# Mixer B of a two-layer encoder: probabilities times values as split products with the values' two parts in one 128-column operand

## The chip, the cores and the metric

The kernel runs on one core of a Trainium2 chip. The metric is the device time of one launch in microseconds (us); lower is better. Engines are named as in the profile: PE is the TensorE matmul engine and PEld its weight loads, DVE is VectorE, ACT is ScalarE, POOL is GpSimd, SP issues most DMAs. Each engine runs its own instructions strictly in the order in which they were written, and waits at the head of its queue until what that instruction reads is there.

## The reference, cut to what matters

Two layers of the same form run over a sequence of 512 tokens with 1024 features. A layer projects its input `u` with one wide matrix into mixer A (dilated windows), mixer B (grouped attention), gates and merge gates; the two mixers' outputs are projected, merged, projected again and normalised. The change is in mixer B: 8 query heads share 2 key/value heads of 64 features, and every query sees all 512 keys.

```
def one_block(qblk):
    logits = jnp.einsum('bqkge,bske->bkgqs', qblk, k, preferred_element_type=jnp.float32) * (HEAD_DIM ** -0.5)
    p = jax.nn.softmax(logits, axis=-1).astype(v.dtype)
    return jnp.einsum('bkgqs,bske->bqkge', p, v)
```

All data are 32-bit floats. The kernel computes most products in a rounded 32-bit type (`fp32r`, F32R in the code) that PE takes at full rate: it splits each operand into a rounded high part and the low part that is left, and adds two or three products of parts.

## The kernel before

**Weights.** The fill work of a layer is one stream of weight chunks. A chunk is split in four pieces by `split_piece`: ACT copies a piece of `raw` into `wh` (L175, rounds it), DVE subtracts to get `wl` (L176). One piece is emitted after each unit of fill work (`tick`), a chunk ahead of its use. Units are 12 matmuls of 512 columns (`feature_unit`) or 24 of 256 columns (`token_chunk`), on `uh`, `ul`, `wh`, `wl`, all through the helper `mm` at L90.

**Mixer B** (`mixer_b`) has 16 passes per layer, one per block of 128 queries and pair of heads (e = 0, 1). In each pass

- Q transposes the query block (L613); ACT and DVE make its two parts `qst` (L615, L616),
- L multiplies them with the keys into `L` (128 x 1024 in PSUM); DVE takes the row maximum (L631) and scales it (L634); ACT takes the exponentials of both halves with their sums (L637); DVE inverts the sums (L639) and scales both halves (L641),
- T transposes the probabilities in eight 128x128 blocks into `T` (L663); ACT copies `T` to `pt` (L665),
- V multiplies: for each of the 4 key blocks and each head of the pair one plain 32-bit matmul with a 64-column stationary block of `v`, 128 columns of `pt` moving, the two heads in the two halves of the output's partitions; DVE copies the 128x128 result to `ys` (L655).

**Order.** `pipeline` writes the passes as T(i), Q(i+2), L(i+1), fill, V(i), fill. `weave` puts in between 1.1 units of fill for every step of the mixer, so that most passes carry two units and every fifth carries three. The order on every engine is the order of emission; nothing is sorted later. On DVE a pass therefore reads: row maximum, its scaling, inversion, two scalings, a `wl` piece, the copy of V, now and then the rotation of a query block (L492, L501) or four steps of the adaLN sums (L281, L283), or in layer 1 the normalisation's affine (L1298, L1299), then another `wl` piece, `qst`, and the next row maximum.

**Values.** `b_copy_kv` evacuates keys (`xk`) and values (`v`) of all token blocks from the projection's PSUM result with two ACT copies (L518). In layer 0 it runs once for 4 blocks, right before the key rotation on DVE starts (`k_rotate`: L476 and on, `k_scale`: L543), whose result PE transposes at L597 (`b_keys`). In layer 1 it runs twice for 2 blocks each.

**Buffers.** `pt` has two buffers, `T` and `L` one each, small PSUM results four banks `b` (`B1`).

Of the kernel before, what the change touches and what calls it, by code (L numbers as in the profile page):

```python
# [11 lines left out]
F32 = mybir.dt.float32  # L12
F32R = mybir.dt.float32r
AF = mybir.ActivationFunctionType
# [24 lines left out]
def trunk_kernel(ctx, tc, x, c, rel_table, ln_g, ln_b, w_ada, b_ada, w_in, b_gate,  # L39
                 q_norm_g, k_norm_g, w_pa, w_pb, w_o, rope, buckets, out):  # L40
    nc = tc.nc
    pe, act, dve, pool, sp = nc.tensor, nc.scalar, nc.vector, nc.gpsimd, nc.sync
# [5 lines left out]
    ring = ctx.enter_context(tc.tile_pool(name="ring", bufs=2))  # L48
# [7 lines left out]
    def fresh(p):  # L56
        uid[0] += 1
        return f"{p}{uid[0]}"
# [21 lines left out]
    G = Slots(one, "g", NG, [128, 512])  # L80
    B1 = Slots(psum, "b", 4, [128, 512])

    def big(tag):
        return psum.tile([128, 1024], F32, tag=tag, name=fresh(tag))
# [4 lines left out]
    def mm(o, l, r, start, stop):  # L89
        pe.matmul(o, l, r, start=start, stop=stop, skip_group_check=True)  # L90
# [123 lines left out]
    idn = one.tile([128, 128], F32, name="idn")  # L214
# [255 lines left out]
    small = ring  # L470
# [41 lines left out]

    def b_copy_kv(r0, nr, o, st):

        if "v" not in st:
            st["v"], st["xk"] = G.get(), G.get()
        for n, c in (("xk", 0), ("v", 128)):
            act.activation(st[n].rearrange("p (r d) -> p r d", r=4)[:, r0:r0 + nr], o[:, :, c:c + 128], AF.Copy)  # L518

    def b_copy_q(ch, rp, o, st):  # L520
        xq = st["xq", ch, rp] = G.get()
# [83 lines left out]
    def mixer_b(st, ys):  # L605
        subs = [(2 * rp + r, 2 * ch + hp) for rp in range(2) for ch in range(2) for r in range(2) for hp in range(2)]

        def Q(i):
            r, hp = subs[i]
            qd = st["qd", hp // 2, r].rearrange("p (h f) -> p h f", h=4)  # L610
            o = B1.get()
            for e in range(2):
                pe.transpose(o[:, 128 * e:128 * e + 128], qd[:, 2 * (hp % 2) + e], idn)  # L613
            q = small.tile([128, 2, 256], F32R, tag="qst", name=fresh("qst"))
            act.activation(q[:, 0], o[:, 0:256], AF.Copy)  # L615
            dve.tensor_sub(q[:, 1], o[:, 0:256], q[:, 0].bitcast(F32))  # L616
            B1.put(o)
            st["q", i] = q
            if hp % 2:
                G.put(st["qd", hp // 2, r])  # L620

        def L(i):
            q_factors(st)
            r, hp = subs[i]
            ks, q = st["ks", hp // 2], st.pop(("q", i))
            lg = big("L")
            for e in range(2):
                for j in range(2):
                    mm(lg[:, 512 * e:512 * e + 512], q[:, j, 128 * e:128 * e + 128], ks, j == 0, j == 1)
            sm = small.tile([128, 3, 2], F32, tag="bst", name=fresh("bst"))  # L630
            dve.tensor_reduce(out=sm[:, 0], in_=lg.rearrange("p (e k) -> p e k", e=2), op=OP.max, axis=AX.X, negate=True)  # L631
            at = 16 * (hp // 2) + 4 * r + 2 * (hp % 2)
            f = st["qn"][:, 1, at:at + 2]
            dve.tensor_mul(sm[:, 0], sm[:, 0], f)  # L634
            p = tmp4("s")
            for e in range(2):
                act.activation(p[:, 512 * e:512 * e + 512], lg[:, 512 * e:512 * e + 512], AF.Exp,  # L637
                               scale=f[:, e:e + 1], bias=sm[:, 0, e:e + 1], accum_out=sm[:, 1, e:e + 1])
            dve.reciprocal(sm[:, 2], sm[:, 1])  # L639
            for e in range(2):  # L640
                dve.tensor_scalar(p[:, 512 * e:512 * e + 512], p[:, 512 * e:512 * e + 512], sm[:, 2, e:e + 1], None, op0=MUL)  # L641
            st["p", i] = p

        def T(i):
            st["pt", i] = transpose_p(st.pop(("p", i)))

        def V(i):
            r, hp = subs[i]
            pt = st.pop(("pt", i)).rearrange("p (e k q) -> p e k q", e=2, k=4)
            v = st["v"].rearrange("p (r h d) -> p r h d", r=4, h=2)  # L650
            o = B1.get()
            for k in range(4):
                for e in range(2):
                    mm(o[64 * e:64 * e + 64, 0:128], v[:, k, hp // 2], pt[:, e, k], k == 0, k == 3)
            dve.tensor_copy(ys[hp][:, 128 * r:128 * r + 128], o[:, 0:128])  # L655
            B1.put(o)

        yield from pipeline(len(subs), Q, L, T, V, lambda i: True, st["more"])

    def transpose_p(p):  # L660
        t = big("T")
        for j in range(8):
            pe.transpose(t[:, 128 * j:128 * j + 128], p[:, 128 * j:128 * j + 128], idn)  # L663
        pt = tmp4("pt")
        act.activation(pt, t, AF.Copy)  # L665
        return pt
# [619 lines left out]
    for l in range(DEPTH):  # L1286
# [30 lines left out]
        def main():  # L1317
            yield from b_prepare(st, deque([keep] * 8 if l else []))
            yield from mixer_b(st, yb)
            b_done["b"] = True  # L1320
            G.put(st["v"], st["ks", 0], st["ks", 1])
            yield from mixer_a(st, 0, ya, deque([lambda: None] * 4 + [lambda: load_bias(st, 1)]))
            yield from mixer_a(st, 1, ya)

# [73 lines left out]
```

## Time and profile before

| | us |
|---|---|
| median of 3 runs | 1197.84 (1197.66 to 1198.01) |
| the profiled execution, own time | 1199.13 |
| its span, first to last instruction | 1197.0 |
| PE busy in the span | 1163.0 |
| DVE busy | 675.4 |
| ACT busy | 531.1 |

Mixer B occupies about 80 to 230 us (layer 0) and 660 to 810 us (layer 1) of the span. A busy time is the union of an engine's instructions. A matmul's shown duration includes its passage through the array; what it costs in a full stream is the distance from its start to the next one's start. On DVE too, an instruction may start a little before the one ahead of it has ended, and its price in a row of instructions is the distance of starts.

### The profile page before, as it was taken

Reading aid. Unit: us, or ns where it says so; the run is one execution under the profiler, and the core shown is the slowest. Engines: PE = TensorE matmul, PEld = TensorE weight load, DVE = VectorE, ACT = ScalarE, POOL = GpSimd, SP = SyncE. Lnnn points to the kernel's source line nnn. Section 1 sums busy time; section 2 is a strip of 40 time slices with the busy share of each in tenths; the row PEclk is TensorE's granted clock in tenths of the full one; section 3 lists DMA queues with packets and bytes.
Section 4 is the critical chain, followed back from the end, with each engine's and each line's share of the span. In section 5 each row is a group of like instructions: output and inputs, shape, how many; then the busy total and the mean of one; then the engine's idle time right before and its main releaser. Section 6 shows DMA issues by size and latency. Waiting matters only on the chain.

```text
span 1197.0 us, 19187 instructions
## 1 busy us (share of the span) xinstructions
PE 1163.0 (97%) x7491; PEld 998.2 (83%) x7491; DVE 675.4 (56%) x1582; ACT 531.1 (44%) x1112; POOL 54.0 (5%) x85
## 2 busy tenths in 40 slices
PE   7899999999999999999989999999999999999996
PEld 6888888888887787888989888888878778888896
DVE  6776766655455365336755667664333533843477
ACT  2364544444554454323275545544554553533320
POOL 0021000001000000000002001000000000000000
PEclk9999999999999999999999999999999999999998
DMA  9935433546343243334522326335232223323331
GB/s 280 294 116 150 123 109 117 150 133 185 103 128 120 59 129 96 90 104 150 170 71 71 114 91 182 112 107 167 83 114 85 88 73 114 116 88 106 123 107 71
DMA packets 161314, 146.31 MB, mean 122 GB/s; under 512 B 8942, under 2 KB 149078, under 8 KB 161224
## 3 DMA queue, kind: packets, MB, share of 16 engines
q1 hardware_dynamic: 159176, 139.71, 38.5%
q0 software_dynamic: 2048, 5.38, 1.9%
q8 instruction: 59, 0.97, 0.3%
q14 instruction: 31, 0.25, 0.1%
HBM read 134.87 MB, written 8.62 MB: 120 GB/s over the span
## 4 chain that ended last, share of the span: by engine, by line
PE 88%; DVE 6%; ACT 2%; DMA 1%; issue 1%; SPq 1%; POOL 0%; DVEq 0%; ACTq 0%
PE b L90 75%; PE L L90 6%; PE T L663 5%; DVE acc L283 1%; PE T L90 1%; DMA raw<-in_w_ada_dram 1%; PE b L613 1%; DVE wl L176 1%; ACT g L948 0%; DMA s<-in_w_in_dram 0%; SPq L999 0%; DVE g L1252 0%; DVE g L1258 0%; ACT g L1271 0%; DVE wl L1023 0%
## 5 line engine op out<-in xcount | busy, mean ns | idle before, releaser
L176 DVE TENSOR_TENSOR wl<-raw,wh 128x512 fp32r<-128x512 f32 x304 | 205.1, 687 | 286.1 <-ACT wh L175 286.1
L90 PE MATMUL b<-uh,wh 128*128 128x512 f32 x768 | 308.4, 402 | 0.6 <-ACT g L423 0.6
L90 PE MATMUL b<-uh,wl 128*128 128x512 f32 x768 | 299.5, 390 | 1.7 <-DVE wl L176 1.7
L90 PE MATMUL b<-ul,wh 128*128 128x512 f32 x768 | 300.0, 391 | 0.0
L175 ACT ACTIVATE wh<-raw 128x512 fp32r<-128x512 f32 x304 | 179.9, 622 | 32.7 <-issue 24.8
L90 PEld LDWEIGHTS b<-uh,wh 128*128 128x128 f32 x768 | 144.0, 188 | 43.6 <-issue 12.0
L90 PEld LDWEIGHTS b<-uh,wl 128*128 128x128 f32 x768 | 144.2, 188 | 33.8 <-DVE wl L176 2.5
L90 PEld LDWEIGHTS b<-ul,wh 128*128 128x128 f32 x768 | 144.3, 188 | 27.6
L90 PE MATMUL b<-wh,uh 128*128 128x256 f32 x416 | 120.8, 290 | 0.0
L90 PE MATMUL b<-wl,uh 128*128 128x256 f32 x416 | 117.7, 283 | 0.0
L90 PE MATMUL b<-wh,ul 128*128 128x256 f32 x416 | 117.6, 283 | 0.0
L665 ACT ACTIVATE pt<-T 128x1024 f32<-128x1024 f32 x64 | 65.4, 1022 | 73.3 <-PE T L663 70.3
L738 ACT ACTIVATE s<-s,ast 128x256 f32<-128x256 f32 x128 | 63.5, 497 | 68.3 <-DVE ast L733 62.9
L283 DVE SCALAR_TENSOR_TENSOR acc<-raw,sc,acc 128x256 f32<-128x256 f32 x168 | 81.3, 484 | 8.4 <-DMA raw<-in_w_ada_dram 3.2
L90 PEld LDWEIGHTS b<-wh,uh 128*128 128x128 f32 x416 | 79.5, 191 | 4.8 <-issue 3.6
L90 PEld LDWEIGHTS b<-wl,uh 128*128 128x128 f32 x416 | 79.5, 191 | 0.8 <-DVE wl L176 0.2
L90 PEld LDWEIGHTS b<-wh,ul 128*128 128x128 f32 x416 | 79.4, 191 | 0.0
L90 PE MATMUL b<-g,wh 128*128 128x512 f32 x256 | 79.2, 391 | 0.0
L637 ACT ACTIVATE s<-L,bst,qn 128x512 f32<-128x512 f32 x64 | 49.2, 773 | 65.9 <-DVE bst L634 65.9
L90 PE MATMUL b<-wh,g 128*128 128x256 f32 x384 | 71.4, 284 | 0.7 <-DVE g L1191 0.5
L90 PE MATMUL b<-pt,g 128*64 128x128 f32 x1024 | 70.0, 279 | 0.0
L90 PEld LDWEIGHTS b<-pt,g 128*64 128x64 f32 x1024 | 54.6, 136 | 17.7 <-issue 13.7
(177 smaller groups left out, 1615.5 us busy)
## 6 DMA issues: line engine op xcount, KB each, us to landing
raw<-in_w_in_dram SPq DMA_DIRECT2D x126, 512.0 KB, 4.1
raw<-in_w_ada_dram SPq DMA_DIRECT2D x96, 256.0 KB, 3.9
raw<-in_w_o_dram SPq DMA_DIRECT2D x16, 512.0 KB
g<-in_x_dram SPq DMA_DIRECT2D x16, 256.0 KB, 5.5
vph<-g SPq DMA_DIRECT2D x16, 256.0 KB, 2.1
g<-vph SPq DMA_DIRECT2D x16, 256.0 KB, 6.0
g<-frow SPq DMA_DIRECT2D x32, 128.0 KB, 3.1
raw<-in_w_pa_dram SPq DMA_DIRECT2D x8, 512.0 KB, 3.5
```

What stands on the lines that cost most here:

```text
L90: pe.matmul(o, l, r, start=start, stop=stop, skip_group_check=True)
L175: act.activation(hi[:, d], raw[:, s], AF.Copy)
L176: dve.tensor_sub(lo[:, d], raw[:, s], hi[:, d].bitcast(F32))
L283: dve.scalar_tensor_tensor(a, raw[:, k], col, a, op0=MUL, op1=ADD)
L613: pe.transpose(o[:, 128 * e:128 * e + 128], qd[:, 2 * (hp % 2) + e], idn)
L637: act.activation(p[:, 512 * e:512 * e + 512], lg[:, 512 * e:512 * e + 512], AF.Exp, scale=f[:, e:e + 1], bias=sm[:, 0, e:e + 1], accum_out ...
L663: pe.transpose(t[:, 128 * j:128 * j + 128], p[:, 128 * j:128 * j + 128], idn)
L665: act.activation(pt, t, AF.Copy)
L738: act.activation(p4[:, e, b], p4[:, e, b], AF.Exp, bias=sm[:, e, b:b + 1], accum_out=s_t[:, rb, e, 1:2])
```

## The change

`b_copy_kv` keeps no plain `v` any more. It makes two tiles `v0`, `v1` (two token blocks each) in which every head has 128 columns: 64 of the rounded high part (ACT copy), 64 of the low part (DVE subtraction). T evacuates to two tiles of the ring `pt`: ACT's copy is now the rounded high part, and DVE subtracts to make the low part, 128 x 1024, out of PSUM. V does 8 matmuls with a 128-column stationary block and 256 moving columns (both heads at once): for each key block the high and the low `pt`. The output has the products with the values' high part in partitions 0 to 63, those with the low part in 64 to 127. The two halves are added at the evacuation: ACT copies the lower half (64 x 256) to a small tile `wot`, and DVE adds, once per head, 64x128 each, the second one into partitions 64 to 127 of `ys`.

```
 def b_copy_kv(r0, nr, o, st):
-        if "v" not in st:
-            st["v"], st["xk"] = G.get(), G.get()
-        for n, c in (("xk", 0), ("v", 128)):
-            act.activation(st[n].rearrange("p (r d) -> p r d", r=4)[:, r0:r0 + nr], o[:, :, c:c + 128], AF.Copy)
+        if "xk" not in st:
+            st["xk"], st["v", 0], st["v", 1] = G.get(), G.get(F32R), G.get(F32R)
+        act.activation(st["xk"].rearrange("p (r d) -> p r d", r=4)[:, r0:r0 + nr], o[:, :, 0:128], AF.Copy)
+        for r in range(r0, r0 + nr, 2):
+            v = st["v", r // 2].rearrange("p (r h s d) -> p r h s d", r=2, h=2, s=2)
+            ov = o[:, r - r0:r - r0 + 2, 128:256].rearrange("p r (h d) -> p r h d", h=2)
+            act.activation(v[:, :, :, 0], ov, AF.Copy)
+            dve.tensor_sub(v[:, :, :, 1], ov, v[:, :, :, 0].bitcast(F32))
...
 def T(i):
-            st["pt", i] = transpose_p(st.pop(("p", i)))
+            t = big("T")
+            p = st.pop(("p", i))
+            for j in range(8):
+                pe.transpose(t[:, 128 * j:128 * j + 128], p[:, 128 * j:128 * j + 128], idn)
+            hl = [ring.tile([128, 1024], F32R, tag="pt", name=fresh("pt")) for _ in range(2)]
+            act.activation(hl[0], t, AF.Copy)
+            dve.tensor_sub(hl[1], t, hl[0].bitcast(F32))
+            st["pt", i] = [x.rearrange("p (e k q) -> p e k q", e=2, k=4) for x in hl]
 def V(i):
             r, hp = subs[i]
-            pt = st.pop(("pt", i)).rearrange("p (e k q) -> p e k q", e=2, k=4)
-            v = st["v"].rearrange("p (r h d) -> p r h d", r=4, h=2)
+            pt = st.pop(("pt", i))
             o = B1.get()
+            ov = o[:, 0:256].rearrange("p (e q) -> p e q", e=2)
             for k in range(4):
-                for e in range(2):
-                    mm(o[64 * e:64 * e + 64, 0:128], v[:, k, hp // 2], pt[:, e, k], k == 0, k == 3)
-            dve.tensor_copy(ys[hp][:, 128 * r:128 * r + 128], o[:, 0:128])
+                v = st["v", k // 2].rearrange("p (r h f) -> p r h f", r=2, h=2)[:, k % 2, hp // 2]
+                for j in range(2):
+                    mm(ov, v, pt[j][:, :, k], k == 0 and j == 0, k == 3 and j == 1)
+            t = small.tile([128, 256], F32, tag="wot", name=fresh("wot"))[0:64]
+            act.activation(t, o[64:128, 0:256], AF.Copy)
+            for e in range(2):
+                dve.tensor_add(ys[hp][64 * e:64 * e + 64, 128 * r:128 * r + 128], o[0:64, 128 * e:128 * e + 128],
+                               t[:, 128 * e:128 * e + 128])
```

PE, the first V of layer 0 with a fill matmul before and after it. Here `b_1107` and `b_1113` are the result of V, `pt` the transposed probabilities, `g` a value tile; before:

```order
L90 MATMUL b_1042<-ul,wh_825 128x512
L90 MATMUL b_1042<-uh,wl_826 128x512
L90 MATMUL b_1107<-pt_1066,g_720 64x128 x8
L90 MATMUL b_1126<-uh,wh_1006 128x512
L90 MATMUL b_1126<-ul,wh_1006 128x512
```

and now:

```order
L90 MATMUL b_1046<-uh,wl_830 128x512
L90 MATMUL b_1113<-pt_1070,g_721 128x256
L90 MATMUL b_1113<-pt_1071,g_721 128x256
L90 MATMUL b_1113<-pt_1070,g_721 128x256
L90 MATMUL b_1113<-pt_1071,g_721 128x256
L90 MATMUL b_1113<-pt_1070,g_722 128x256
L90 MATMUL b_1113<-pt_1071,g_722 128x256
L90 MATMUL b_1113<-pt_1070,g_722 128x256
L90 MATMUL b_1113<-pt_1071,g_722 128x256
L90 MATMUL b_1135<-uh,wh_1010 128x512
```

The place in the order is the same; eight matmuls of 128 columns into 64 partitions have become eight of 256 columns into 128 partitions.

DVE, from one row maximum (`bst<-L`) to the next in layer 1, in a pass that also rotates a query block (`gt`: rotary tables); before:

```order
L631 TENSOR_REDUCE bst_7145<-L_7140 128x2
L634 TENSOR_TENSOR bst_7145<-bst_7145,qn_6241 128x2
L639 RECIPROCAL bst_7145<-bst_7145 128x2
L641 TENSOR_SCALAR s_7148<-s_7148,bst_7145 128x512 x2
L176 TENSOR_TENSOR wl_7079<-raw_6772,wh_7078 128x512
L655 COPY g_6409<-b_7170 128x128
L492 TENSOR_TENSOR g_6396<-g_6396,gt_88 128x512
L492 TENSOR_TENSOR s_7180<-s_7180,gt_89 128x512
L501 TENSOR_TENSOR g_7185<-g_6396,s_7180 128x512
L501 TENSOR_TENSOR g_7186<-g_6396,s_7180 128x512
L176 TENSOR_TENSOR wl_7079<-raw_6772,wh_7078 128x512
L616 TENSOR_TENSOR qst_7221<-b_7218,qst_7221 128x256
```

and the same pass now, from the two scalings on:

```order
L645 TENSOR_SCALAR s_7267<-s_7267,bst_7264 128x512 x2
L176 TENSOR_TENSOR wl_7193<-raw_6871,wh_7192 128x512
L671 TENSOR_TENSOR g_6496<-b_7289,wot_7298 64x128 x2
L492 TENSOR_TENSOR g_6483<-g_6483,gt_88 128x512
L492 TENSOR_TENSOR s_7302<-s_7302,gt_89 128x512
L501 TENSOR_TENSOR g_7307<-g_6483,s_7302 128x512
L501 TENSOR_TENSOR g_7308<-g_6483,s_7302 128x512
L176 TENSOR_TENSOR wl_7193<-raw_6871,wh_7192 128x512
L655 TENSOR_TENSOR pt_7339<-T_7329,pt_7338 128x1024
L620 TENSOR_TENSOR qst_7345<-b_7342,qst_7345 128x256
L635 TENSOR_REDUCE bst_7353<-L_7348 128x2
```

Two additions stand where the copy stood, and the new subtraction of 1024 columns stands ahead of `qst` and of the next row maximum.

DVE at the start of layer 0, behind the last weight pieces of the first projection; before:

```order
L176 TENSOR_TENSOR wl_694<-raw_621,wh_693 128x512 x2
L467 TENSOR_TENSOR gt_88<-ropec,grow 128x256
L467 TENSOR_TENSOR gt_89<-ropec,grow 128x256
L467 TENSOR_TENSOR gt_90<-ropec,grow 128x256
L467 TENSOR_TENSOR gt_91<-ropec,grow 128x256
L476 TENSOR_REDUCE nst_760<-s_761 128x8
```

and now:

```order
L176 TENSOR_TENSOR wl_694<-raw_621,wh_693 128x512 x2
L522 TENSOR_TENSOR g_721<-L_102,g_721 128x4x64
L522 TENSOR_TENSOR g_722<-L_102,g_722 128x4x64
L467 TENSOR_TENSOR gt_88<-ropec,grow 128x256
L467 TENSOR_TENSOR gt_89<-ropec,grow 128x256
L467 TENSOR_TENSOR gt_90<-ropec,grow 128x256
L467 TENSOR_TENSOR gt_91<-ropec,grow 128x256
L476 TENSOR_REDUCE nst_764<-s_765 128x8
```

The two subtractions of the values stand ahead of the four rotary tables, and so ahead of the sums over the keys (`nst`).

## Rows read from the trace of the kernel before

**Rows 1.** The page, part 1: busy us (share of the span), instructions.

```profile
PE 1163.0 (97%) x7491; PEld 998.2 (83%) x7491; DVE 675.4 (56%) x1582; ACT 531.1 (44%) x1112; POOL 54.0 (5%) x85
```

**Rows 2.** Stretches of 14 passes: length, busy PE, PEld, DVE, ACT, POOL, clock, DMA.

```profile
93.30:228.60 135.30, 135.27 (x938) 116.22 (x937) 90.39 (x194) 66.93 (x136) 1.73 (x3) 1.00 0.42 122
671.00:802.50 131.50, 131.50 (x889) 111.56 (x888) 87.78 (x180) 66.07 (x135) 5.07 (x8) 1.00 0.42 125
```

**Rows 3.** DVE groups in 93.30:228.60: count | busy us, mean ns | idle before, releaser.

```profile
L639 DVE RECIPROCAL bst<-bst 128x2 f32<-128x2 f32 x14 | 2.3, 166 | 24.9 <-ACT s L637 24.9
```

**Rows 4.** Timeline of PE around a V: start, duration, line, operation, operands.

```profile
94.85 0.39 PE L90 MATMUL b<-ul,wh 128*128 128x512 f32 x1
95.07 0.39 PE L90 MATMUL b<-uh,wl 128*128 128x512 f32 x1
95.39 1.09 PE L90 MATMUL b<-pt,g 128*64 128x128 f32 x16
...
96.75 0.40 PE L90 MATMUL b<-ul,wh 128*128 128x512 f32 x1
```

**Rows 5.** Timeline of PE, consecutive fill matmuls of 256 columns.

```profile
165.31 0.28 PE L90 MATMUL b<-wh,uh 128*128 128x256 f32 x1
165.42 0.28 PE L90 MATMUL b<-wl,uh 128*128 128x256 f32 x1
```

**Rows 6.** Timeline of DVE, one pass of layer 1.

```profile
726.78 1.22 DVE L631 TENSOR_REDUCE bst<-L 128x2 f32<-128x1024 f32 x1
...
730.18 0.88 DVE L641 TENSOR_SCALAR s<-s,bst 128x512 f32<-128x512 f32 x2
730.98 0.69 DVE L176 TENSOR_TENSOR wl<-raw,wh 128x512 fp32r<-128x512 f32 x1
731.59 0.28 DVE L655 COPY g<-b 128x128 f32<-128x128 f32 x1
731.79 0.68 DVE L492 TENSOR_TENSOR g<-g,gt 128x512 f32<-128x512 f32 x1
...
734.98 0.42 DVE L616 TENSOR_TENSOR qst<-b,qst 128x256 fp32r<-128x256 f32 x1
735.32 1.22 DVE L631 TENSOR_REDUCE bst<-L 128x2 f32<-128x1024 f32 x1
```

**Rows 7.** Timeline of DVE: the first output starts at partition 0, the second at 64.

```profile
69.76 0.69 DVE L176 TENSOR_TENSOR wl<-raw,wh 128x512 fp32r<-128x512 f32 x1
70.46 1.30 DVE L600 TENSOR_TENSOR g<-b,g 64x512 fp32r<-64x512 f32 x2
```

**Rows 8.** Timeline of PE and ACT: transposes, their evacuation, V, the next transposes.

```profile
723.78 1.03 PE L663 MATMUL T<-idn,s 128*128 128x128 f32 x8
...
724.91 1.03 ACT L665 ACTIVATE pt<-T 128x1024 f32<-128x1024 f32 x1 [2.54 <-PE T L663]
...
728.64 1.09 PE L90 MATMUL b<-pt,g 128*64 128x128 f32 x16
...
732.51 1.03 PE L663 MATMUL T<-idn,s 128*128 128x128 f32 x8
```

**Rows 9.** Timeline of DVE and PE: a low part that PE waits for.

```profile
166.68 0.68 DVE L176 TENSOR_TENSOR wl<-raw,wh 128x512 fp32r<-128x512 f32 x1
...
167.10 0.28 PE L90 MATMUL b<-wh,uh 128*128 128x256 f32 x1
167.41 0.38 PE L90 MATMUL b<-wl,uh 128*128 128x256 f32 x1
```

**Rows 10.** Timeline of ACT, DVE and PE at the start of layer 0.

```profile
61.67 1.42 DVE L467 TENSOR_TENSOR gt<-ropec,grow 128x256 f32<-128x256 f32 x4
...
62.10 1.09 ACT L518 ACTIVATE g<-L 128x512 f32<-128x512 f32 x2 [1.92 <-PE L L90]
...
63.74 0.69 DVE L476 TENSOR_REDUCE nst<-s 128x8 f32<-128x512 f32 x1 [0.65 <-ACT s L475]
...
68.07 1.77 PE L597 MATMUL b<-idn,g 128*128 128x128 f32 x8 [0.25 <-DVE g L543]
```

More of the change, by code (lines that the diff above doesn't have):

```diff
@@ L1320, in main @@
             b_done["b"] = True
-            G.put(st["v"], st["ks", 0], st["ks", 1])
+            G.put(st["v", 0], st["v", 1], st["ks", 0], st["ks", 1])
             yield from mixer_a(st, 0, ya, deque([lambda: None] * 4 + [lambda: load_bias(st, 1)]))
```

## The prediction

> **What bounds the kernel now.** I read the page's first part, then the stretches of mixer B, then single passes. PE is busy for 1163 of 1197 us, DVE for 675 [rows 1]. In the two stretches that hold 14 of a layer's 16 passes each, PE is busy for 135.27 of 135.30 us and for all of 131.50, at a granted clock of 1.00 [rows 2]: what PE is given there, it does without a gap, so a shorter V shortens the kernel, if nothing else gets late. The next thing to see is how much room DVE has. It is busy for 90.39 and 87.78 us there [rows 2]. But it takes its instructions in order, and in every pass it stands at the inversion of the sums until ACT has the exponentials: 24.9 us in 14 passes, 1.78 each, the same in both layers [rows 3]. With them DVE is taken for 115.3 of 135.3 and 112.7 of 131.5 us. A pass with a rotation shows it from near: from one row maximum to the next, 8.54 us [rows 6], there is no idle time but that wait. So PE sets the time, and DVE is behind it by only 20.0 and 18.8 us in 14 passes, 1.3 to 1.4 us a pass.
>
> **The change part by part.**
>
> *V on PE.* Before, from the start of the last fill matmul ahead of V to the start of the second one behind it are 96.75 - 95.07 = 1.68 us [rows 4]. A 512-column matmul in the full stream takes 0.227 (94.85 to 95.07 is such a step, 0.227 the median of 660 like it), two of them 0.454, so V costs 1.226. The same difference at the other 31 V's is 1.22 to 1.32. After, V is eight matmuls of 128 stationary and 256 moving columns in the same rounded type as the fill's, and those go 0.12 us apart [rows 5]: 0.96. They fill the whole array as their neighbours do, so I add no edge. PE gains 0.265 a pass, 32 x 0.265 = **8.5 us**.
>
> *The low part of `pt` on DVE.* A subtraction of 256 columns out of PSUM takes 0.42 us [rows 6], one of 512 columns 0.69 [rows 7], so 1.05 ns a column; 1024 columns make 0.69 + 512 x 1.05 = 1.23, near the row maximum, which reads the same 1024 columns in 1.22 [rows 6]. In a row of instructions the next one starts 0.08 earlier than that (0.61 after a 0.69 [rows 6]): 1.14. The bounds: 1.0 if the fixed part shrinks, 1.3 if it costs as two of 512.
>
> *The evacuation of V.* The copy costs 0.20 (731.59 to 731.79 [rows 6]). Each addition has the same 128 columns out of PSUM: 0.20 more. The second one writes partitions 64 to 127 behind one that writes 0 to 63. What that does a pair of rows shows: the instruction that writes from partition 64 starts 0.70 after a 0.69 one, with no overlap [rows 7], where otherwise 0.61 lie between [rows 6]. Two such steps (there and back) cost 0.16. So +0.36, bounds 0.20 and 0.36. The Trainium skill, VectorE: DVE Perf Modes, section on two Vector instructions with no wait between them, states a rule for this: an instruction is held until all earlier ones have finished when its output starts in another group of 32 partitions than the last output. By that rule the two additions are held as the row shows it; if neither held, the sum below would be 3.2 us less.
>
> Together DVE gets 1.50 us more in each pass, where it had 1.3 to 1.4 to spare, and PE is to become 0.265 shorter. ACT's copy of 64x256 lies on an engine with half its time free (66.93 of 135.30 [rows 2]); I cost it at nothing in itself.
>
> *The stretches as a sum.* DVE needs 115.3 + 14 x 1.50 = 136.3 and 133.7 us; PE needs 135.3 - 3.7 = 131.6 and 127.8. DVE is 4.7 and 5.9 us over, 10.6, against a gain on PE of 8.5: **DVE becomes the engine that sets the pace of mixer B**, and even if it never waited for anything but the exponentials, 2.1 us would be lost.
>
> *It will wait.* The queue has two more conditions. (a) The new subtraction cannot start before ACT has copied `T`: transposes at 723.78, the copy from 724.91 for 1.03 [rows 8], so 2.2 us after the transposes start; with 1.14 and 0.34 for `qst` the next row maximum cannot start earlier than 3.7 after them. (b) The next transposes need the first scaled half: from the row maximum at 726.78 to the end of the first scaling, 730.18 + 0.44 [rows 6], and 0.1 to wake PE, 3.95. I walked the passes by these: row maximum = the later of the last one + DVE's need, and transposes + 3.7; transposes = the later of PE's need and row maximum + 3.95; V not ahead of the end of the subtraction. Where DVE had a wait of its own behind the transposes before (a `wl` piece on ACT's copy), that stays. PE's needs are the distances of the 32 starts of transposes (732.51 - 723.78 is one [rows 8]) less 0.265, DVE's its busy time in the pass plus 1.78 plus 1.50. For passes 2 to 15, in us:
>
> Layer 0, PE 11.2, 9.2, 8.7, 8.5, 8.9, 11.2, 9.3, 8.7, 8.6, 8.9, 11.2, 8.8, 8.8, 8.9; DVE 10.0, 11.7, 9.6, 9.9, 9.3, 9.6, 12.4, 7.8, 9.2, 9.3, 9.5, 10.0, 9.3, 9.0. PE then stands for 0, 0.5, 0.9, 1.4, 0.8, 0, 3.6, 0, 0, 0.4, 0, 0.9, 0.5, 0.5: 9.5.
> Layer 1, PE 8.5, 11.2, 8.6, 8.7, 8.6, 8.5, 11.2, 8.9, 8.7, 8.7, 8.5, 11.6, 8.5, 8.4; DVE 10.0, 8.9, 9.5, 10.0, 8.8, 10.4, 10.0, 11.3, 9.2, 10.4, 8.8, 9.4, 10.3, 7.1. PE stands for 0.7, 0, 0, 0.3, 0.2, 1.9, 0.9, 0.3, 0.4, 1.7, 0.4, 0, 0, 0: 6.8.
>
> The 3.6 is a low part of the weights: already before, a matmul at 167.41 waits for the piece that DVE began at 166.68, 0.2 us over the 0.12 of the stream [rows 9, 5]; that piece stands behind the scalings in DVE's queue and gets later with them. Elsewhere the pieces come well ahead of their use. Mixer B: 16.3 - 8.5 = **+7.8 us**. With 1.0 for the subtraction and 0.20 for the additions the same walk gives +2.0, with 1.3 and 0.36 it gives +11.
>
> *Values' parts at the start.* In layer 0 the two new subtractions stand ahead of the four rotary tables on DVE. ACT copies from 62.10 on, two copies in 1.09 [rows 10]; now three of the same columns in all, so the last subtraction ends near 63.7, the tables take 1.42 from there [rows 10], 65.1, and the sums over the keys start 1.4 later than at 63.74. PE's transposes of the keys already wait for that chain (0.25 at 68.07 [rows 10]): **+1.4 us**. In layer 1 DVE stands idle at that place until the keys come, longer than the subtractions take: nothing.
>
> Sum: 1199.13 (the profiled execution, span 1197.0) - 8.5 + 16.3 + 1.4 = 1208.3. That execution is 1.3 above the median of 1197.84, so against the median **1207.0 us**. A measurement of this kernel can tell about 0.2%, 2.4 us, from no change.
>
> **The rivals.**
> *The gain arrives.* If the work added to DVE is near 1.0 us a pass, it fits in the 38.8 us that DVE has to spare: at 1.1 (131.6 - 115.3 over 14 passes is 1.16, 127.8 - 112.7 is 1.08) both engines need the same, and below it PE sets the time again. For it: DVE has other idle time in many passes, and a late DVE no longer waits for PE. Against it: rows price the work at 1.5, and the order leaves 6 long passes of three units whose room the short ones cannot borrow. 1197.8 - 8.5 + 1.4 = 1190.7; chance 0.14.
> *They cancel.* Some of the waits go, PE stands for about 7 to 9 us in all: 1195.5 to 1200.2; chance 0.13.
> *DVE's other waits stay.* If its waits for `wh` and for `qst` do not shrink as it gets late, about half of its 20 us a layer stay: some 8 us more, 1211 to 1220; chance 0.12.
> *V does not get cheaper.* The change would not do what it says if the matmuls with `pt` were not paced as the fill's: at the 0.227 of 512 columns V is 1.8, and 32 x 0.6 = 19 us are lost on PE, part of them under DVE's time: 1215 or more; chance 0.03.
>
> **How the numbers follow.** My forecast, DVE sets the pace of mixer B, 1200.3 to 1212: 0.58. Slower in all 0.58 + 0.12 + 0.03 = 0.73, same 0.13, faster 0.14. The range from 1196.5 to 1216 leaves out the first rival (0.14), and some of the two dear ones and of the cancelling one (0.07).
>
> **What would show it.** In the profile after: V with starts 0.12 apart, 0.96 in all; DVE's subtraction `pt<-T` at 1.23 each, 32 of them; DVE busy in mixer B up by 21 us a layer to some 80% of it; PE no longer without gaps there, with waits of T on the scalings (`s`) and of V on `pt`, both released by DVE, 12 to 18 us in all; the transposes of the keys in layer 0 at 69.4. If PE has no gaps in mixer B and the time is under 1195, the step with DVE's queue is wrong; if PE has gaps but they end with ACT or a DMA, the mechanism is another. Outside mixer B and that start nothing should move.

## The result and the profile after

The changed kernel takes **1215.74 us** (median of 4 runs, 1214.60 to 1216.74) against 1197.75 of the kernel before (1197.55 to 1198.01): 1.0148 times as long, 95% interval 1.0136 to 1.0161, 18.0 us more. The forecast was 1207.0, with a range of 1196.5 to 1216.0: slower as forecast, inside the range by 0.3 us, but 8.7 us above the forecast and above the 1200.3 to 1212 of its own case. That it still lies inside the range is owed to the room that the range left for dearer cases.

The page of the profile after, part 1 (against [rows 1]) and the chain of part 4, with the chain of the kernel before ahead of it:

```profile
PE 88%; DVE 6%; ACT 2%; DMA 1%; issue 1%; SPq 1%; POOL 0%; DVEq 0%; ACTq 0%
```

```profile
PE 1164.7 (96%) x7235; PEld 1005.7 (83%) x7235; DVE 722.6 (60%) x1650; ACT 543.1 (45%) x1145; POOL 53.7 (4%) x85
...
PE 66%; DVE 21%; ACT 6%; issue 3%; DMA 2%; SPq 1%; POOL 0%; DVEq 0%; ACTq 0%
```

DVE has 47 us more to do, and a fifth of the chain that ends last is DVE, against 6% before. PE has 256 matmul records fewer (a plain 32-bit matmul of V stood for two, x16 in [rows 4]), and its busy time is still not shorter: the ends of matmuls are modelled, and a slower clock makes them longer (0.41 instead of 0.28 us for 256 columns at 72.41), so the idle time in the next rows understates how long PE stands. The stretches of mixer B that answer to [rows 2]:

```profile
93.30:240.00 146.70, 139.33 (x847) 122.66 (x846) 110.80 (x223) 73.36 (x152) 4.92 (x8) 0.99 0.41 119
681.00:820.00 139.00, 133.14 (x786) 114.76 (x785) 108.66 (x209) 72.67 (x151) 5.05 (x8) 1.00 0.40 120
```

Where PE had no gap before, it is idle for 7.4 and 5.9 us, and DVE has 20 us more. What PE waits for there (engine, line, what it waited for: us, times, longest) in 90 to 247, layer 0:

```profile
PE b L90 <- DVE pt L655: 4.9, 6, 1.6
PE b L90 <- ACT wh L175: 1.1, 1, 1.1
PE T L652 <- DVE s L645: 0.8, 3, 0.3
PE b L90 <- DVE wl L176: 0.7, 1, 0.7
```

and in 670 to 830, layer 1:

```profile
PE b L90 <- DVE pt L655: 4.0, 5, 1.4
PE T L652 <- DVE s L645: 1.7, 6, 0.4
```

V waits for the low part of the probabilities, and the transposes for the scaling, both on DVE. The starts of the 64 groups of transposes show where the 16.6 us of the two spans lie:

| from | to | before | after | more |
|---|---|---|---|---|
| 0 | first transposes, layer 0 | 90.55 | 93.76 | 3.21 |
| there | 16th transposes of layer 0 | 143.29 | 151.53 | 8.24 |
| there | first transposes, layer 1 | 434.31 | 434.05 | -0.26 |
| there | 16th transposes of layer 1 | 140.95 | 146.17 | 5.22 |
| there | end | 387.9 | 388.1 | 0.2 |

All of it is in mixer B and at the start of layer 0. A pass in which nothing waits is 0.25 to 0.29 shorter than before, the 0.265 of the prediction. PE's timeline around a V (against [rows 4]):

```profile
98.28 0.39 PE L90 MATMUL b<-uh,wl 128*128 128x512 f32 x1
98.51 1.12 PE L90 MATMUL b<-pt,g 128*128 128x256 f32 x8
99.46 0.40 PE L90 MATMUL b<-uh,wh 128*128 128x512 f32 x1
```

V takes 0.95 from its start to the start of the next fill matmul. The gain is there; it is given back by the waits around it. DVE's queue in the pass of layer 1 that answers to [rows 6]:

```profile
730.79 1.22 DVE L635 TENSOR_REDUCE bst<-L 128x2 f32<-128x1024 f32 x1
...
733.96 0.17 DVE L643 RECIPROCAL bst<-bst 128x2 f32<-128x2 f32 x1 [1.76 <-ACT s L641]
734.16 0.88 DVE L645 TENSOR_SCALAR s<-s,bst 128x512 f32<-128x512 f32 x2
...
735.57 0.57 DVE L671 TENSOR_TENSOR g<-b,wot 64x128 f32<-64x128 f32 x2
736.18 0.69 DVE L1315 TENSOR_TENSOR g<-g,g 128x512 f32<-128x512 f32 x1
...
739.94 1.22 DVE L655 TENSOR_TENSOR pt<-T,pt 128x1024 fp32r<-128x1024 f32 x1
741.08 0.41 DVE L620 TENSOR_TENSOR qst<-b,qst 128x256 fp32r<-128x256 f32 x1
741.41 1.22 DVE L635 TENSOR_REDUCE bst<-L 128x2 f32<-128x1024 f32 x1
```

and PE's transposes that follow it:

```profile
744.67 0.39 PE L90 MATMUL b<-uh,wl 128*128 128x512 f32 x1
745.41 1.07 PE L652 MATMUL T<-idn,s 128*128 128x128 f32 x8 [0.35 <-DVE s L645]
```

The two additions take 0.57 to 0.61, the low part 1.14 to the next start, and from one row maximum to the next 10.62 us pass, without idle time but the wait for the exponentials. The row maximum at 741.41 is followed by the transposes at 745.41, 4.00 later; in 15 of the 32 such distances it is 3.9 to 4.1, against 4.8 and more before. That is the loop that sets the pace: row maximum, exponentials, scaling, transposes.

### The profile page after: what moved, and what is told of

It is laid out like the page before. It is cut to its first block, busy times and chain, and to the rows that moved or that the text cites. A ratio compares the mean times of both kernels' runs of the same rounds, so it can differ in the third digit from the quotient of the medians.

```text
span 1213.6 us, 18752 instructions
## 1 busy us (share of the span) xinstructions
PE 1164.7 (96%) x7235; PEld 1005.7 (83%) x7235; DVE 722.6 (60%) x1650; ACT 543.1 (45%) x1145; POOL 53.7 (4%) x85
## 4 chain that ended last, share of the span: by engine, by line
PE 66%; DVE 21%; ACT 6%; issue 3%; DMA 2%; SPq 1%; POOL 0%; DVEq 0%; ACTq 0%
PE b L90 57%; PE L L90 4%; ACT s L641 3%; DVE acc L283 3%; DVE wl L176 3%; DVE pt L655 3%; DVE bst L635 3%; PE T L680 2%; DMA raw<-in_w_ada_dram 2%; DVE s L645 2%; DVE g L671 1%; PE T L90 1%; PE T L652 1%; DVE qst L620 1%; SPq L1016 1%
## 5 line engine op out<-in xcount | busy, mean ns | idle before, releaser
L176 DVE TENSOR_TENSOR wl<-raw,wh 128x512 fp32r<-128x512 f32 x304 | 205.2, 687 | 265.5 <-ACT wh L175 265.1
L283 DVE SCALAR_TENSOR_TENSOR acc<-raw,sc,acc 128x256 f32<-128x256 f32 x168 | 81.4, 484 | 10.3 <-DMA raw<-in_w_ada_dram 5.2
L90 PE MATMUL b<-pt,g 128*64 128x128 f32 (+1 forms) x768 | 75.0, 283 | 9.2 <-DVE pt L655 8.9
L90 PEld LDWEIGHTS b<-pt,g 128*64 128x64 f32 (+1 forms) x768 | 61.6, 154 | 23.7 <-DVE pt L655 12.8
L90 PEld LDWEIGHTS b<-wh,g 128*128 128x128 f32 x384 | 60.5, 192 | 1.6 <-DVE g L1208 0.9
```

The lines of the kernel that those rows point to most:

```text
L176: dve.tensor_sub(lo[:, d], raw[:, s], hi[:, d].bitcast(F32))
L283: dve.scalar_tensor_tensor(a, raw[:, k], col, a, op0=MUL, op1=ADD)
```

## The experiments

Times stand against the 1215.74 of the changed kernel and the kernel before, which was run beside each (1197.69 to 1198.52). "Step" is the distance from one pass's group of transposes to the next one's, less the same distance in the kernel before; "pass n" is the distance that begins at the nth group.

### 1. Without the low part

```diff
-hl = [ring.tile([128, 1024], F32R, tag="pt", name=fresh("pt")) for _ in range(2)]
+hl = [ring.tile([128, 1024], F32R, tag="pt", name=fresh("pt"))] * 2
 act.activation(hl[0], t, AF.Copy)
-dve.tensor_sub(hl[1], t, hl[0].bitcast(F32))
```

> The changed kernel without DVE's subtraction of the low part in mixer B: V's eight matmuls use the high part twice (the low part of the probabilities is left out of the result), so PE's work, ACT's copies and the two additions stay as they are. Theory, DVE's queue sets the pace: DVE gets 1.14 us a pass back, keeps +0.36 for the additions, and by the walk of the passes mixer B takes 7.5 us less than in the kernel before (one stall of 1.0 us is left, ahead of the tenth pass of layer 0), while the start of layer 0 stays 3.2 us late: 1197.8 - 7.5 + 3.2 = 1193.5 us, and no half-clock stretch inside mixer B. Rival, the loss comes from what is left in (the evacuation through ACT and two additions that hold V's bank longer, or V itself): at least 10 of the 13.4 us lost in the passes stay, 1207 us or more.

1193.57 us (0.9959 times before, 0.9945 to 0.9973). The steps are -0.21 to -0.30 in all passes but one, pass 8 of layer 0, which stands for 0.95 (the stall of 1.0 that is expected there); no clock below 1.00 inside mixer B. So V's gain is as priced, the copy on ACT and the additions alone cost PE nothing but that one stall, and the subtraction is what turns the gain into a loss. The edit also leaves out the second `pt` tile of a pass, and that is not the cause: in the changed kernel ACT's copy of `T` starts 1.07 to 1.22 us after the transposes in 29 of 32 passes, as in the kernel before. That the time meets the 1193.5 so closely is in part luck: in its profile mixer B's first transposes come 3.9 late instead of 3.2, and the stretch between the two layers' mixers B is 1.8 shorter than before, which no term had.

### 2. Before, with the subtraction alone

```diff
 pt = tmp4("pt")
 act.activation(pt, t, AF.Copy)
+low = tmp4("pt")
+dve.tensor_sub(low, t, pt)
```

> The kernel before with one thing added: in each pass of mixer B, DVE subtracts the copied transposes from the transposes in PSUM into a tile that nobody reads (1024 columns, as in the changed kernel); V, the copy of V and the values stay as before. Theory, DVE has 1.3 to 1.4 us of room a pass on average but some passes have less: by the walk PE stands for 0.8, 2.3, 0.5 us at single passes, 4.8 in all: 1202.6 us, up to 1204.2 if the clock falls behind the longest stall. Rival A, the room is enough: 1197.8 to 1198.5. Rival B, the subtraction alone makes all of the loss of the stretches (21.6 us of stalls in the changed kernel): 1210 or more.

1204.72 us (1.0056, 1.0041 to 1.0071), 6.6 more than before. PE stands at single passes, as the walk has it: 0.85 at pass 5 and 2.57 at pass 8 of layer 0, 0.43 and 0.80 at passes 7 and 11 of layer 1. Without pass 9 (1.06, at half the clock, below) the steps add up to 5.7 against 4.8. The subtraction alone (1.14 a pass) does not fit, although it is less than the mean room of 1.3 to 1.4: the room of single passes is what counts. It costs less alone than with the additions and a PE that is 0.265 faster.

### 3. The values' low parts later

```diff
 act.activation(v[:, :, :, 0], ov, AF.Copy)
-dve.tensor_sub(v[:, :, :, 1], ov, v[:, :, :, 0].bitcast(F32))
+if nr == 4:
+    st.setdefault("vlow", []).append((v, ov))
+else:
+    dve.tensor_sub(v[:, :, :, 1], ov, v[:, :, :, 0].bitcast(F32))
...
 b_keys(st)
+for v, ov in st.pop("vlow", ()):
+    dve.tensor_sub(v[:, :, :, 1], ov, v[:, :, :, 0].bitcast(F32))
```

> The changed kernel with the two subtractions of the values' low parts in layer 0 moved behind the keys' subtractions on DVE; all work stays. Theory: the transposes of the keys start at 68.1 again as in the kernel before (69.85 in the changed one), PE's gap ahead of them falls from 2.1 to 0.3 us, and with it goes the stretch at 0.5 of the clock behind it, so that the first transposes of mixer B are 3.2 us earlier and the time falls by 3.2: 1212.5 us. Rival A, the gap moves but the clock falls for another reason: 1.8 us, 1213.9. Rival B, the two values copies of ACT are what delays the chain: no more than 0.5 us, 1215.2.

1213.52 us, 2.2 less. The transposes of the keys start at 68.60 in a run whose rotary tables are already 0.47 late ([rows 10], 62.14 against 61.67), with a gap of 0.31 in place of 2.07, and the clock stays at 1.00. The first transposes of mixer B come 2.02 earlier, not 3.2: the 0.47, and 0.5 more at the wait on ACT at 88. The time falls by about as much only because two other changes cancel: mixer B of layer 0 takes 1.5 more (the clock is at 0.50 in two stretches there, from 173.8 and from 221.6, and pass 13 stands 1.9 longer), and the stretch from there to layer 1's first transposes takes 1.5 less. Rival B is out; what the clock costs the next run shows alone.

### 4. The gap filled

```diff
 o = B1.get()
+if kv == 0 and not warmed:
+    warmed.append(1)
+    warm(o, 8)
```

> The changed kernel with eight 128-column matmuls of constants on PE ahead of the first transposes of the keys in layer 0 (some 1.8 us of work in PE's gap of 2.1 us, into a bank that the transposes then overwrite); all else stays. Theory: PE's gap is what the clock falls after; with the gap filled the stretch at 0.5 behind it goes, and the first transposes of mixer B come 1.4 us earlier with the keys' transposes still at 69.85: 1214.3 us. Rival, the transposes of the keys and the matmuls behind them are slow for another reason, or the clock falls there all the same: 1215.7 us, with the half-clock stretch from 70.8 still there.

PE's timeline of the changed kernel and then of this one at the keys:

```profile
67.50 0.28 PE L90 MATMUL b<-wh,ul 128*128 128x256 f32 x1
69.85 2.33 PE L601 MATMUL b<-idn,g 128*128 128x128 f32 x8 [2.07 <-DVE g L547]
```

```profile
67.60 1.95 PE L90 MATMUL b<-ones,idn 128*128 128x128 f32 x16
69.82 1.45 PE L606 MATMUL b<-idn,g 128*128 128x128 f32 x5 [0.28 <-DVE g L547]
```

and the stretch behind, length, busy PE, PEld, DVE, ACT, POOL, granted clock, again first the changed kernel:

```profile
70.00:74.00 4.00, 3.98 (x18) 3.42 (x18) 3.94 (x9) 1.80 (x4) 2.06 (x1) 0.60 0.00 0
```

```profile
70.00:74.00 4.00, 3.98 (x30) 3.45 (x30) 3.94 (x9) 1.69 (x4) 2.06 (x1) 1.00 0.00 0
```

The keys start at the same time, the granted clock behind them is 1.00 instead of 0.60 on average (30 matmuls against 18 in 4 us), and the first transposes of mixer B come 1.43 us earlier, as expected. The time falls by more, to 1211.90: in this profile the clock also stays up behind the last gap ahead of layer 1 (in the changed kernel it falls there, at 633.97), the stretch between the two layers' mixers B is 1.5 shorter, and pass 13 of layer 0 is 0.8 shorter.

### 5. The scalings on ACT

```diff
-dve.tensor_scalar(p[:, 512 * e:512 * e + 512], p[:, 512 * e:512 * e + 512], sm[:, 2, e:e + 1], None, op0=MUL)
+act.activation(p[:, 512 * e:512 * e + 512], p[:, 512 * e:512 * e + 512], AF.Copy, scale=sm[:, 2, e:e + 1])
```

> The changed kernel with the two scalings of a pass by the inverse sums moved from DVE to ACT (the same 2 x 512 columns, ACT's copy with a scale). Theory, DVE's queue sets the pace: DVE gets 0.8 us a pass back of the 1.5 added; ACT does it in place, some 0.3 us later than DVE did, since one copy of 512 columns takes 0.6 there. By the walk mixer B then takes 4.6 us less than in the kernel before (2.3 to 5.7 by how late the first scaled half is), the start stays 3.2 late: 1197.8 - 4.6 + 3.2 = 1196.4, range 1195 to 1199; PE's waits on the low part go, and its stall ahead of the tenth pass of layer 0 gets shorter. Rival, the loss is a chain from the transposes through ACT's copy to V and to the next transposes, whatever is queued on DVE: ACT takes 1.2 us a pass more and the scaling lies later in that chain, so nothing is won: 1215 or more.

1255.60 us (1.0475, 1.0457 to 1.0492): 40 more, where 19 less were expected. DVE's waits in 96 to 240, the changed kernel first:

```profile
DVE bst L643 <- ACT s L641: 24.6, 14, 1.8
DVE pt L655 <- ACT pt L654: 5.4, 2, 2.7
...
DVE wl L176 <- ACT wh L175: 1.3, 1, 1.3
```

```profile
DVE wl L176 <- ACT wh L175: 27.8, 15, 2.4
DVE bst L643 <- ACT s L641: 21.2, 12, 1.8
DVE pt L655 <- ACT pt L654: 5.8, 2, 3.1
```

DVE does less (102.2 us busy from the first to the 16th transposes of layer 0, against 114.3) and waits more: its next entry, a low part of the weights, needs a copy `wh` that ACT now makes behind the two scalings, and DVE stands up to 2.4 us with everything queued behind. The scalings had been the work that covered that copy. The time is on the rival's side, and a part of its chain did grow: ACT's copy of `T` starts 2.3 us or more after the transposes in 21 of 32 passes, against 1.07 to 1.22 in 29 of 32. But DVE's subtraction waits for that copy hardly more than in the changed kernel (5.8 against 5.4), and the shortest distances from a row maximum to the transposes are 4.14 against 3.9; what is new is the wait of 27.8 for `wh`. DVE's waits count like its work, and the theory had left out what ACT queues behind the scalings. That DVE's queue and not the rival's chain makes the 40 us is read from these rows and not shown, since the edit loads both engines' queues; experiments 7 to 12 shorten DVE's queue and leave that chain as it is.

### 6. The weights' low parts on POOL

```diff
-dve.tensor_sub(lo[:, d], raw[:, s], hi[:, d].bitcast(F32))
+if state.get("in_b"):
+    pool.tensor_tensor(out=lo[:, d], in0=raw[:, s], in1=hi[:, d].bitcast(F32), op=SUB)
+else:
+    dve.tensor_sub(lo[:, d], raw[:, s], hi[:, d].bitcast(F32))
```

> The changed kernel with the low parts of the weights (31 subtractions of 512 columns in 14 passes of layer 0) done by POOL instead of DVE as long as mixer B runs; DVE keeps the low parts of the probabilities and the additions. Theory, DVE's queue sets the pace: DVE gets some 1.3 us a pass back, by the walk mixer B takes 7.9 us less than in the kernel before, the start stays 3.2 late: 1197.8 - 7.9 + 3.2 = 1193.1, up to 1197 where POOL's slower subtractions come late for a fill. Rival A, the loss does not hang on what else DVE does: 1212 or more. Rival B, POOL slows DVE's instructions beside it (its subtractions and DVE's get longer in the rows): between the two, with DVE's low part of the probabilities above its 1.22 us.

1231.43 us (1.0271, 1.0256 to 1.0286). DVE's groups in 660 to 815, count, busy us, mean ns; the changed kernel, then this one:

```profile
L655 DVE TENSOR_TENSOR pt<-T,pt 128x1024 fp32r<-128x1024 f32 x14 | 17.1, 1219 | 0.9 <-ACT pt L654 0.9
L645 DVE TENSOR_SCALAR s<-s,bst 128x512 f32<-128x512 f32 x28 | 12.4, 483 | 0.5
...
L1316 DVE TENSOR_TENSOR g<-g,g 128x512 f32<-128x512 f32 x8 | 5.5, 692 | 0.3
```

```profile
L648 DVE TENSOR_SCALAR s<-s,bst 128x512 f32<-128x512 f32 x26 | 18.8, 765 | 0.5
...
L658 DVE TENSOR_TENSOR pt<-T,pt 128x1024 fp32r<-128x1024 f32 x13 | 15.8, 1218 | 3.0 <-ACT pt L657 2.9
L1319 DVE TENSOR_TENSOR g<-g,g 128x512 f32<-128x512 f32 x8 | 9.4, 1178 | 0.3
```

DVE's busy time does not fall (114.75 us from the first to the 16th transposes of layer 1 against 112.65, although the 33 weights' subtractions that it had there are POOL's): the scalings go from 483 to 765 ns, additions with both operands in SBUF from 692 to 1178, while the subtraction that reads PSUM stays at 1219. Rival B is the mechanism, though not by the instruction that it named, and the time is worse than its bounds. The mean hides two kinds: of the 30 scalings there 22 still take 0.48 to 0.49 us, and 8 take 1.51 to 1.54, about 1 us more, where a subtraction on POOL takes 1.35 on average. The Trainium skill, SBUF — State Buffer, section SBUF: two separate sides, has a rule for it: DVE and GpSimd share a pair of ports, which DVE needs for two inputs in SBUF or in a two-port mode, and the later one waits for the whole instruction. The rows agree, on which instructions get longer and on which don't; the rotation's additions (L504), which also read two inputs in SBUF, never ran beside one of POOL's subtractions and stay at 689. In layer 0 DVE also waits 8.9 us for loads of the modulation's sums (the adaLN sums `acc`, L281 and L283; in 96 to 240, against 1.7), so that not all of the loss there is the ports'.

### 7 and 8. The modulation's sums behind mixer B, after and before

```diff
-ADA = 7
+ADA = 17
...
-        ada_at.setdefault((1, 9 + i), []).append((1, 8 + i // 2, i % 2))
+        ada_at.setdefault((1, 19 + i), []).append((1, 8 + i // 2, i % 2))
```

`ADA` is the chunk of weights at which the sums written in layer 0 begin, and `ADS` chunks hold six of their loads.

> The changed kernel with the partial sums of the modulation on DVE (acc, 0.36 to 0.49 us apiece, 42 in layer 0 and 21 in layer 1 beside mixer B) and the loads that feed them moved behind mixer B into the stretches of mixer A and later; nothing is left out, and the low parts, the additions and the order T, Q, L, V of the passes stay. Theory, the sum of DVE's queue decides: by the walk without these instructions mixer B takes 0.7 us more than in the kernel before instead of 7.8, 7.1 less: 1215.7 - 7.1 = 1208.6 us; the waits of PE on the low part get fewer, and the start stays 3.2 late. Rival A, it is the new chain from the transposes through ACT's copy and the subtraction to the next row maximum, whatever else is queued: 1214.5 or more. Rival B, the sums cost the same where they go: DVE or the loads bind there, 1215 or more with the loss behind mixer B.

> The kernel before with the same move of the modulation's partial sums and their loads behind mixer B. Theory, PE sets the pace of mixer B in the kernel before and DVE has room in both places: no change, 1197.8 us (1196.5 to 1199), so that what the same move gives the changed kernel is due to the change. Rival, the move itself is worth something (loads, banks, transposes of the sums): 1195 or less, or 1201 or more.

1204.73 us for the changed kernel (11.0 less) and 1206.30 for the kernel before (1.0069, 1.0054 to 1.0084). The theory on the kernel before is wrong, for a reason away from mixer B. PE's timeline of the kernel before with this edit:

```profile
453.18 0.98 PE L90 MATMUL b<-ones,acc 128*128 128x1 f32 x4 [6.40 <-DVE acc L283]
```

Some of the sums now fall into the z stage, where DVE multiplies the gates in (about 443 to 456 us). One waits there for a load (3.41 us), the last one stands in DVE's queue behind the gates, PE waits 6.4 us for it (7.45 in the changed kernel), and the granted clock is at 0.5 behind it. In mixer B the move does what the theory says: of the changed kernel's stalls of 21.6 us some 3.9 are left beside the kernel before with the same move (the 15 distances of a layer are 2.8 and 1.2 shorter there, against 15 x 0.265), and pass 8 of layer 0 falls from 3.63 to 0.7. Against the kernel before with the same move the changed kernel's median is now 1.6 us lower; its four executions spread from 1202.75 to 1206.77, around the 1205.90 to 1206.72 of the other, so this run does not show that it is faster.

### 9. Three edits together

> The changed kernel with three edits together: the partial sums of the modulation behind mixer B, the two subtractions of the values' low parts of layer 0 behind the keys' subtractions, and eight 128-column matmuls of constants ahead of the first transposes of the keys; nothing is left out. Theory, the parts add up: 7.1 in mixer B, 1.8 of the keys' wait and 1.4 of the clock behind it: 1215.7 - 10.3 = 1205.4 us, still slower than before, since the low parts of the weights and the rotations stay in DVE's queue. Rival, the gap at the start was cover for what comes late behind it: with the keys on time the stalls at the first passes grow by as much, 1208 or more.

1203.42 us: 1.3 less than with the sums alone, against 3.2 expected; the executions of the two overlap. In the profiles the first transposes come 0.73 later than in the kernel before, 1.95 earlier than there, with the clock at 1.00, and no stall of mixer B takes that back: the rival is out. The wait ahead of the z stage (444.4 to 451.3) is in it as before, and is the larger part of what is left.

### 10 and 11. The sums placed to end before the z stage

```diff
-ADA = 17
-ADS = 4
+ADA = 14
+ADS = 3
```

The other lines are those of experiments 3, 4 and 7; the kernel before gets `ADA`, `ADS` and `19 + i` alone.

> The three edits of the run before together again, with the partial sums of layer 0 begun three chunks of weights earlier and two instead of one and a half of them to a chunk, so that they end before the z stage, where in the run before PE waits 6.9 us for one of them (444.4 to 451.3) and the clock is at 0.5 behind it. Theory: that wait and the half-clock stretch go (some 7 us, and 1.5 to 3 of the clock), a sum or two come back beside the last passes of mixer B of layer 0 (0.5 to 1 each): 1203.4 - 8 = 1195.5 us, under the kernel before by 0.2%. Rival, the sums are late wherever they are denser, since the loads that feed them share the weights' five buffers: a wait of the same size elsewhere, 1201 or more.

> The kernel before with the same placing of the modulation's partial sums as in the combined kernel of this call, and nothing else. Theory: with the wait ahead of the z stage gone the move is worth nothing to the kernel before, which PE bounds in mixer B: 1197 to 1199 us, so that the combined kernel's difference from it, -2 to -3 us, is what the change brings when DVE has room. Rival, the move itself is a gain for both: 1195 or less.

1196.17 us (0.9985, 0.9976 to 0.9994), and 1197.39 for the kernel before with the same placing (0.9998, 0.9989 to 1.0007). The executions of the two do not overlap (up to 1197.01, from 1197.20). The wait of 6.9 us is gone, and the placing itself is worth nothing to the kernel before, so what it gives the changed kernel is DVE's room. Of the 20.1 us between the profiles of the changed kernel and of this one the passes of mixer B make 20.6, the start 2.7, and the stretch between the layers takes 2.8 back.

### 12. One chunk later, without the constants' matmuls

`ADA` is 15, and the lines of experiment 4 are out.

> The combined kernel of the call before with two mends: the partial sums of layer 0 begin one chunk of weights later, so that none stands ahead of the last low part of mixer B (there PE waits 1.28 us for it at 233.2), and without the eight matmuls of constants, which end 1 us after the keys are ready now that the values' low parts are out of their way. Theory: 1.3 to 1.6 us for the wait and up to 0.7 for the keys: 1196.2 - 2 = 1194.2 us, 0.3% under the kernel before. Rival, the last sums now run into the z stage, where DVE has long rows of its own: a new wait of 1 us or more at 430 to 455, and 1196 or more; or the clock falls at the start without the matmuls: 1195.6.

**1193.47 us** (0.9965, 0.9951 to 0.9978), faster than both kernels: 4.2 under the one before, 22.3 under the changed one, with the same mathematics. Its largest waits of PE inside mixer B are 0.7 on the low part and 0.9 in three pieces on the scalings; the wait of 1.28 at 233 is gone, no new one stands at 430 to 455, and the first transposes come 0.42 later than in the kernel before. Of the 8.5 us of V half arrives; 3.8 are left as stalls of the passes, against experiment 11. The kernel before with the sums begun at this chunk was not run.

## Why the prediction was right, and where it was too low

*V on PE*, 0.96: measured 0.95, and -0.25 to -0.29 in each free pass. Right.

*The low part*, 1.23 and 1.14 in a row: 1219 ns, and 1.13 to 1.14 to the next start in 30 of 32. Right.

*The additions*, +0.36: two starts 0.29 apart with 0.28 of work, and 0.32 to the next; 0.61 against 0.20 for the copy, +0.41. The second addition is held, as the rule on two Vector instructions with no wait between them in the Trainium skill, VectorE: DVE Perf Modes, has it. Right within 0.05.

*The walk.* How long PE stands in passes 2 to 15, predicted, and measured as step + 0.265:

| | predicted | measured |
|---|---|---|
| layer 0 | 0, 0.5, 0.9, 1.4, 0.8, 0, 3.6, 0, 0, 0.4, 0, 0.9, 0.5, 0.5: 9.5 | 0, 1.1, 0.8, 1.5, 0.4, 0.1, 3.6, 1.6, 0, 0, 0, 2.0, 0.7, 0.5: 12.3 |
| layer 1 | 0.7, 0, 0, 0.3, 0.2, 1.9, 0.9, 0.3, 0.4, 1.7, 0.4, 0, 0, 0: 6.8 | 0.8, 0.1, 0, 0.4, 0.2, 2.2, 1.0, 0.2, 0.4, 1.9, 0.3, 0.5, 1.3, 0.1: 9.3 |

In most passes place and size are those of the prediction. The 3.6 of pass 8 is met by luck: the prediction has one low part of the weights there, and PE stands at three places:

```profile
170.53 1.10 PE L90 MATMUL b<-pt,g 128*128 128x256 f32 x7 [1.30 <-DVE pt L655]
...
174.91 0.38 PE L90 MATMUL b<-wh,uh 128*128 128x256 f32 x1 [1.13 <-ACT wh L175]
175.96 0.39 PE L90 MATMUL b<-wl,uh 128*128 128x256 f32 x1 [0.66 <-DVE wl L176]
```

The middle one ends with ACT, but starts with DVE as well: ACT makes this `wh` at 174.23 behind the exponentials, for which it had stood 6.03 us until DVE had the row maximum (172.23).

Three other passes make 4.0 of the missing 5.3. Pass 9 of layer 0 (1.6) stands behind the longest stall, at half the clock; that the clock makes all of the 1.6 is read from this row, not from a run of its own:

```profile
176.60:180.00 3.40, 3.40 (x15) 3.21 (x15) 0.76 (x2) 1.30 (x2) 0.00 (x0) 0.50 0.55 154
```

In pass 13 of layer 0 and pass 14 of layer 1 (2.0 and 1.3) DVE waits for loads of the modulation's sums, here ahead of the low part of each:

```profile
219.11 2.04 DVE L283 SCALAR_TENSOR_TENSOR acc<-raw,sc,acc 128x256 f32<-128x256 f32 x4 [1.41 <-DMA raw<-in_w_ada_dram]
...
809.83 0.35 DVE L281 TENSOR_SCALAR acc<-raw,sc 128x256 f32<-128x256 f32 x1 [2.17 <-DMA raw<-in_w_ada_dram]
```

The walk had no term for a wait of DVE for loads: in the kernel before there is only one of 0.2 us in mixer B. It is DVE's own lateness that comes back here: ahead of these two loads the queue that issues them waits 7.0 and 7.3 us for a weights' subtraction of DVE (L176). This comes near the rival "DVE's other waits stay", whose range of 1211 to 1220 holds the result; but the two waits that this rival names did shrink (in layer 0 for `wh` from 11.3 to 1.3 us, for `qst` from 8.6 to none), so its time fits for another reason than its own.

*The start*, +1.4: the keys are 1.78 late. DVE and ACT wait for each other there:

```profile
62.97 0.42 DVE L522 TENSOR_TENSOR g<-L,g 128x256 fp32r<-128x256 f32 x1 [1.25 <-ACT g L521]
63.84 0.42 DVE L522 TENSOR_TENSOR g<-L,g 128x256 fp32r<-128x256 f32 x1 [0.45 <-ACT g L521]
64.18 1.42 DVE L467 TENSOR_TENSOR gt<-ropec,grow 128x256 f32<-128x256 f32 x4
65.52 0.68 DVE L476 TENSOR_REDUCE nst<-s 128x8 f32<-128x512 f32 x1
```

```profile
63.42 0.38 ACT L521 ACTIVATE g<-L 128x256 fp32r<-128x256 f32 x1 [0.49 <-DVE g L522]
```

ACT's second copy of the values starts at 63.42, when DVE's first subtraction has ended, where the prediction let the copies run on. On top came 1.43 of the clock, which no term had and which experiment 4 shows alone.

So of the 7.3 us between the sum for the profiled execution (1208.3) and its time (1215.59), 0.4 is the start's queue, 3.0 the clock in two places (1.43 at the start, 1.6 in pass 9), and nearly all of the rest PE's other stalls, with 2.4 in the two passes with late loads the largest part. The other 1.3 are the step from the profiled execution of before to its median, which the profiled execution of after does not repeat. So the order, DVE's queue as the bound, was right, and two terms were missing: the price of a gap on PE, of which the sum counted the wait and nothing behind it (3.0), and DVE's waits for loads, put at nothing (2.4). With both the sum would have been 1213.7.

## What to carry to other kernels

Price a change by the room that the engine behind has in each single pass, waits and order included: here the mean room of 1.3 to 1.4 us was nearly the cost of 1.5, and the kernel still got 18 us longer. When that engine becomes the bound, look first at moving work in its queue in time: here a move to ACT cost 40 us and one to POOL 16, while sums moved to a later stage, together with the values' subtractions moved behind the keys', made the change pay. The place that it moves to has waits of its own to be read first: the first one chosen cost 6.4 us.

## What was not expected of the hardware

A gap of some 2 us on PE can cost nearly as much again behind it, and does not always. Ahead of layer 1 PE has several gaps of 1.7 to 1.8 us. The last of them, and the stretch behind it, in the kernel before and then in experiment 3, where the same fall would lie from 633.6 to 637.0:

```profile
622.47 0.74 PE L944 MATMUL b<-idn,g 128*128 128x128 f32 x4 [1.82 <-ACT g L1271]
```

```profile
622.90:626.30 3.40, 3.40 (x19) 3.40 (x17) 1.27 (x2) 2.76 (x7) 0.00 (x0) 0.50 0.03 9
```

```profile
633.16 0.66 PE L966 MATMUL b<-idn,g 128*128 128x128 f32 x4 [1.80 <-ACT g L1293]
```

```profile
635.00:640.00 5.00, 5.00 (x45) 5.00 (x44) 1.88 (x5) 4.55 (x12) 0.00 (x0) 1.00 0.07 12
```

Five of the 14 profiles (before, after, experiments 2, 7 and 12) have the clock at 0.50, 1.2 instead of 2.4 GHz, behind it, the others not; in experiments 1, 3 and 4 the stretch from layer 0's last transposes of mixer B to layer 1's first is 1.8 us shorter than in the kernel before. At half the clock the matmuls of 256 columns start 0.21 apart (72.41, 72.62) instead of 0.12 [rows 5]. What decides it in one execution stays open.
